# A hybrid decoder layer on one core: a group's value products start with the one that needs the last masked copy

## The chip, the cores and the metric

The kernel runs on one core of one Trainium2 chip. The metric is the device time of one execution in microseconds (us). A core has a matrix engine (TensorE, PE in the profile; its weight loads are listed apart as PEld), VectorE (DVE), ScalarE (ACT), GpSimd (POOL) and SyncE (SP), which issues most transfers. Each engine works through its own list of instructions in order and waits on semaphores for the others. Matrix products are written to banks of an accumulation memory called PSUM; DVE and ACT copy them out.

## The reference, cut to what matters

One decoder layer for 2048 tokens of width 1024, in float32. A normalised input is projected into two groups of heads: four recurrent heads (HGRN2) and eight attention heads with two key/value heads. Their outputs are joined, projected and added to the input, then a gated feed-forward part with a short convolution follows, and a last normalisation. The change lies in the attention:

```python
scores = einsum('bnqhgd,bnkhd->bnhgqk', qb, kb) * scale     # a block of 128 queries, 256 keys
scores = where(mask, scores, -inf)                          # causal, window of 128
m = maximum(max(scores, -1), sink)
p = exp(scores - m)
denom = sum(p, -1) + exp(sink - m)
out = einsum('bnhgqk,bnkhd->bnqhgd', p / denom, vb)         # the value products
```

Each block of 128 queries reads its own block of 128 keys and the previous one. The first block of all has no previous one.

## The kernel before, in words

The sequence is worked in two halves of 1024 tokens (`hf` 0 and 1). In each half come the mixing part (the heads), the output projection, the feed-forward products and the down projection. The mixing part lies at about 110 to 380 us and 1190 to 1460 us of the profile. In it, four rounds (`h`, `j` = 0 to 3) pair one recurrent head (`hgrn`, a generator) with one pair of attention heads (`attend`, a generator too: one head of key/value head 0, one of key/value head 1); `hymba_layer` advances the two in turn.

`attend` works on groups of four blocks of 128 queries: `g` = 0 and 1 in a half. So there are 16 groups in all: 2 halves, 4 rounds, 2 groups. For a group, the last part of `attend` does this:

- for each key/value head `kv`, four transposes of the probabilities (L497, tile `ppt`), into one of the two PSUM banks of the pool called "at";
- from that bank two masked copies on DVE (L500): `po`, with the mask of the own block, and `pp`, with the mask of the previous one. A group thus has four masked copies, and DVE makes them in the order po and pp of `kv` 0, po and pp of `kv` 1. The last one is pp of `kv` 1;
- the value products (L508) into one bank of "at" (tile `poT`): for each of the four blocks `i` up to two products (own, previous) for each of the two `kv`, 16 in a group, and 14 in the first group of a round in half 0. The product of `kv` 0 fills partitions 0 to 63 of the bank, that of `kv` 1 fills 64 to 127; own and previous are summed in the bank;
- a copy of the bank by ACT (L512, and L518 in round 3, where DVE also makes a low part, L519). What it writes is read by the output projection of that half.

In the profile every product is two records of LDWEIGHTS and two of MATMUL.

All of the rest of TensorE's work in this part are projections (`unit`, L214: 48 matrix products of 128x512 each, tiles named `f`, `hq`, `q`, `g`, and `pop` for the output projection), and the recurrent head's own products (tiles `pdiag`, `plev`, `pkn`, `pu`, `po` of L671 and L672, `pot`). The masked copy `po` of L500 and the tile `po` of L671 and L672 have one name in the profile and are told apart by their lines.

The order on each engine is not that of the text. A planner plays the traced program through a model of time, gives an engine that is free the earliest traced instruction that is ready in that model, and writes down the order; semaphores are put in afterwards. `tc.issue_after(x)` adds that the instructions traced inside it stand behind `x` on `x`'s engine, without a wait. So a projection of the next head fills TensorE where the model says that the value products aren't ready; at run time the written order holds, whatever is ready then.

Of the kernel before, what the change touches and what calls it, by code (L numbers as in the profile page):

```python
# [17 lines left out]
P = 128  # L18
# [32 lines left out]
def hymba_layer(ctx: ExitStack, tc: tile.TileContext, a: dict, out: bass.AP):  # L51
    nc = tc.nc
# [17 lines left out]
    def ps(kind, name):  # L70
        return spaces[kind].tile([P, 512], F32, tag=kind, name=name)
# [3 lines left out]
    def halves():  # L75
        return [(b, slice(b * 512, (b + 1) * 512)) for b in range(NB)]
# [119 lines left out]
    def unit(src, X, name, order=range(KT), kind="mm", then={}, behind={}, in_turn=False):  # L196


        hi, lo = src if isinstance(src, tuple) else prep(src)
        o = [ps(aux[b] if kind == "aux" else kind, f"{name}{b}") for b in range(NB)]  # L200
        order, mark = list(order), None
        for both in [[h] for h in halves()] if in_turn else [halves()]:
            for i, kt in enumerate(order):
                if i in then:
                    then[i]()
                wh, wl = hi[:, kt * P:(kt + 1) * P], lo[:, kt * P:(kt + 1) * P]
                xh, xl = X[kt]
                if i in behind:
                    mark = marks[behind[i]].ins
                with tc.issue_after(mark) if mark else ExitStack():  # L210
                    for w, x, f, l in ((wh, xh, kt == order[0], False), (wh, xl, False, False),
                                       (wl, xh, False, kt == order[-1])):
                        for b, bs in both:
                            marks["unit"] = nc.tensor.matmul(o[b], w, x[:, bs], start=f, stop=l)  # L214
        return o

    def new_x():
        return (xp.tile([P, HALF], F32R, tag="xh", name="XH", bufs=KT),
                xp.tile([P, HALF], F32R, tag="xl", name="XL", bufs=KT))
# [74 lines left out]
    def slot(name):  # L294
        return hp.tile([P, HALF], F32, tag="m", name=name, bufs=KT)
# [102 lines left out]
    def rows(kv):  # L398
        return slice(kv * HD, (kv + 1) * HD)
# [32 lines left out]
    def attend(hf, j, X, invb, KS, V, mix, p):  # L432

        o = unit(a["w_att"][j], X, "q")
        qT = slot(f"att{j}")
        for b, bs in halves():
            nc.vector.scalar_tensor_tensor(qT[:, bs], o[b], 0.125, invb[:, bs], op0=ALU.mult, op1=ALU.mult)
            nc.scalar.activation(qT[:, bs], qT[:, bs], AF.Identity, bias=C.bq[:, j:j + 1])
        yield
        scs = []  # L440
        for g in range(NB):
            sc = p.tile([P, 2, 4, P], F32, tag="sc", name="sc", bufs=2)
            gs = slice(g * 512, (g + 1) * 512)
            for kv in range(2):
                r, other = rows(kv), rows(1 - kv)

                qh, ql = [p.tile([P, 512], F32R, tag="pp", name=n, bufs=4) for n in ("qh", "ql")]
                nc.scalar.copy(qh[r], qT[r, gs])
                nc.scalar.copy(qh[other], qT[r, gs])
                nc.vector.tensor_tensor(ql[r], qT[r, gs], qh[r].bitcast(F32), op=ALU.subtract)  # L450
                nc.scalar.copy(ql[other], ql[r].bitcast(F32))
                for i0 in (0, 2):
                    pb = ps("at", "psc")
                    first = hf == 0 and g == 0 and i0 == 0
                    for i in range(2):
                        n = g * 4 + i0 + i
                        w0 = 1 if first and i == 0 else 0
                        o = pb[:, i * 256 + w0 * P:(i + 1) * 256]
                        ks = slice((n + w0) * P, (n + 2) * P)
                        for t, qx in enumerate((qh, ql)):  # L460
                            nc.tensor.matmul(o, qx[:, (i0 + i) * P:(i0 + i + 1) * P], KS[:, kv, ks],
                                             start=t == 0, stop=t == 1)
                    pv = pb.rearrange("p (i w k) -> p i w k", i=2, w=2)
                    dst = sc[:, kv, i0:i0 + 2]
                    if first:
                        nc.vector.memset(dst[:, 0], NEG)
                        nc.scalar.copy(dst[:, 1], pv[:, 1, 0])
                    else:
                        nc.scalar.copy(dst, pv[:, :, 0])
                    nc.vector.copy_predicated(  # L470
                        dst, C.own.bitcast(U32).unsqueeze(1).to_broadcast([P, 2, P]), pv[:, :, 1])
            m = p.tile([P, 2, 4], F32, tag="mx", name="m", bufs=2)
            nc.vector.tensor_reduce(m.rearrange("p a b -> p (a b)"),
                                    sc.rearrange("p a b c -> p (a b) c"), axis=AX.X, op=ALU.max)
            sk = C.sinkb[:, j].unsqueeze(2).to_broadcast([P, 2, 4])
            nc.vector.tensor_tensor(m, m, sk, op=ALU.max)
            es = p.tile([P, 2, 4], F32, tag="es", name="es", bufs=2)
            nc.vector.tensor_tensor(es, sk, m, op=ALU.subtract)
            nc.vector.tensor_scalar(m, m, -1.0, None, op0=ALU.mult)
            den = p.tile([P, 2, 4], F32, tag="den", name="den", bufs=2)  # L480
            for kv in range(2):
                for i in range(4):
                    nc.scalar.activation(sc[:, kv, i], sc[:, kv, i], AF.Exp, bias=m[:, kv, i:i + 1],
                                         accum_out=den[:, kv, i:i + 1])
            nc.scalar.activation(es, es, AF.Exp)
            nc.vector.tensor_tensor(den, den, es, op=ALU.add)
            nc.vector.reciprocal(den, den)
            nc.vector.tensor_tensor(sc, sc, den.unsqueeze(3).to_broadcast([P, 2, 4, P]), op=ALU.mult)
            scs.append(sc)
        yield  # L490
        for g, sc in enumerate(scs):
            pm = []
            for kv in range(2):
                pm.append([p.tile([P, 4, P], F32, tag="pp", name=n, bufs=4) for n in ("po", "pp")])
                pt = ps("at", "ppt")
                for i in range(4):
                    nc.tensor.transpose(pt[:, i * P:(i + 1) * P], sc[:, kv, i], ident)  # L497
                ptv = pt.rearrange("p (i q) -> p i q", i=4)
                for dst, mk in zip(pm[kv], (C.ownT, C.prevT)):
                    nc.vector.tensor_tensor(dst, ptv, mk.unsqueeze(1).to_broadcast([P, 4, P]), op=ALU.mult)  # L500
            oT = ps("at", "poT")
            for i in range(4):
                n = g * 4 + i
                noprev = hf == 0 and n == 0
                for prev in range(1 if noprev else 2):
                    for kv in range(2):
                        r = rows(kv)
                        nc.tensor.matmul(oT[r, i * P:(i + 1) * P], V[:, n + 1 - prev, r], pm[kv][prev][:, i],  # L508
                                         start=prev == 0, stop=noprev or prev == 1)
            gs = slice(g * 512, (g + 1) * 512)  # L510
            if j < ATT_J - 1:
                nc.scalar.copy(qT[:, gs], oT)  # L512
                mix[4 + j] = qT
            else:
                if g == 0:
                    mix[4 + j] = new_x()
                h, l = mix[4 + j]
                nc.scalar.copy(h[:, gs], oT)  # L518
                nc.vector.tensor_tensor(l[:, gs], oT, h[:, gs].bitcast(F32), op=ALU.subtract)  # L519
            yield  # L520
# [674 lines left out]
    for hf in range(NH):  # L1195
        X, kv, invb, rs, f0 = nxt
        with ExitStack() as st:
            p = pool(f"mix{hf}", stack=st, reuse_waits="tile")
            KS, V = att_keys(hf, kv, invb, p)
# [3 lines left out]
            for h in range(HG):  # L1203
                hg = hgrn(hf, h, X, invb, vs, WG, mix, p, f0 if h == 0 else None)
                at = attend(hf, h, X, invb, KS, V, mix, p)
                with tc.issue_after(summed.ins) if hf + h == 0 else ExitStack():
                    next(hg)
# [28 lines left out]
        with ExitStack() as st:  # L1236
            p = pool(f"ffn{hf}", stack=st, reuse_waits="tile")
            kept, ops, hs, first, last = out_proj(hf, M, p)
# [63 lines left out]
```

## Time and profile before

| what | us |
|---|---|
| time of the kernel, median of 3 runs | 2175.64 (2173.93 to 2177.19) |
| the profiled execution, time | 2174.83 |
| the profiled execution, span from the first to the last instruction | 2173.1 |
| TensorE busy in 1190 to 1460 us | 266.42 of 270 |
| DVE busy in 1190 to 1460 us | 199.10 of 270 |
| ACT busy in 1190 to 1460 us | 156.88 of 270 |

The span leaves out 1.7 us of the profiled execution. A row of the timeline has the start in us, the time from the first start to the last end of the records that it merges, the engine, line and operation, the tile written and those read, and the number of records (x2). An idle time ahead of the first record and what ended it stand in brackets, where it is long enough. Records on TensorE overlap, because matrix products are pipelined: what one costs is read from its start to the next one's start, not from its duration.

### The profile page before, as it was taken

What the parts mean: (1) busy time and instruction counts of PE and PEld (TensorE: products, weight loads), DVE (VectorE), ACT (ScalarE), POOL (GpSimd) and SP (SyncE); (2) the same over time, 40 slices, a digit from 0 to 9 for tenths busy, and PEclk for the clock granted to TensorE, in tenths of its full rate; (3) what the DMA queues carried; (4) which work ended last, traced back from release to release, by engine and by line L of the source; (5) the groups of instructions that cost most, each with busy time, mean ns of one, the idle gap of its engine ahead of it and who ended that gap; (6) DMA issues with size and microseconds to landing.
All of it is one profiled execution on the core that took longest, in us unless ns stands there. A gap on an engine that the chain in (4) does not pass through costs nothing.

```text
span 2173.1 us, 29038 instructions
## 1 busy us (share of the span) xinstructions
PE 2151.3 (99%) x11136; PEld 1809.6 (83%) x11136; DVE 1659.9 (76%) x2446; ACT 1094.1 (50%) x1902; POOL 6.0 (0%) x28
## 2 busy tenths in 40 slices
PE   9999999999999999999999999999999999999998
PEld 7988987888888888788889889878888888888888
DVE  6677677688887878785866776777978888887766
ACT  6556556564444445335736466555544443444353
POOL 1000000000000000000000000000000000000000
PEclk9999999999999999999999999999999999999999
DMA  4101112413232235964631111124133323259643
GB/s 156 49 30 39 49 40 78 136 59 127 92 126 89 96 117 167 375 223 163 205 127 39 42 37 49 47 70 147 58 116 102 117 82 126 93 190 396 226 142 131
DMA packets 94387, 258.09 MB, mean 119 GB/s; under 512 B 11416, under 2 KB 17576, under 8 KB 94248
## 3 DMA queue, kind: packets, MB, share of 16 engines
q1 hardware_dynamic: 88992, 251.30, 34.2%
q10 hardware_dynamic: 5256, 4.94, 0.8%
q8 instruction: 87, 1.43, 0.3%
q14 instruction: 52, 0.43, 0.1%
HBM read 195.10 MB, written 57.15 MB: 116 GB/s over the span
## 4 chain that ended last, share of the span: by engine, by line
PE 93%; DVE 3%; ACT 2%; DMA 1%; issue 1%; SPq 0%; ACTq 0%; DVEq 0%
PE X L885 7%; PE pop L214 7%; PE X L887 7%; PE X L886 7%; PE hq L214 4%; PE f L214 4%; PE q L214 4%; PE g L214 4%; PE Y L885 4%; PE Y L886 4%; PE Y L887 4%; PE pdx L1098 3%; PE pdx L1096 3%; PE pdx L1097 3%; PE pdy L1096 3%; PE pdy L1097 3%
## 5 line engine op out<-in xcount | busy, mean ns | idle before, releaser
L714 ACT CAST whi<-raw 128x1024 fp32r<-128x1024 f32 x88 | 92.6, 1052 | 109.1 <-PE X L886 68.2
L885 PE MATMUL X<-T,whi 128*128 128x512 f32 x352 | 136.9, 389 | 0.0
L886 PE MATMUL X<-T,whi 128*128 128x512 f32 x352 | 136.9, 389 | 0.0
L887 PE MATMUL X<-T,wlo 128*128 128x512 f32 x352 | 136.9, 389 | 0.0
L980 DVE SCALAR_TENSOR_TENSOR y<-ga,cw,y 128x1024 f32<-128x1024 f32 x88 | 112.4, 1280 | 26.0 <-ACT y L978 26.0
L892 ACT COPY u<-X 128x512 f32<-128x512 f32 x88 | 51.5, 585 | 133.2 <-PE X L887 133.0
L715 DVE TENSOR_TENSOR wlo<-raw,whi 128x1024 fp32r<-128x1024 f32 x88 | 107.2, 1219 | 0.0
L715 DVE TENSOR_TENSOR xld<-raw,xhd 128x1024 fp32r<-128x1024 f32 x72 | 80.9, 1132 | 21.7 <-ACT xhd L714 21.2
L192 ACT CAST whi<-raw 128x1024 fp32r<-128x1024 f32 x57 | 59.9, 1050 | 72.2 <-PE pop L214 28.6
L714 ACT CAST xhd<-raw 128x1024 fp32r<-128x1024 f32 x72 | 69.6, 977 | 47.3 <-DMA raw<-act1T 15.5
L193 DVE TENSOR_TENSOR wlo<-raw,whi 128x1024 fp32r<-128x1024 f32 x57 | 69.2, 1217 | 26.4 <-ACT whi L192 26.3
L214 PE MATMUL pop<-XH,wlo 128*128 128x512 f32 x256 | 85.9, 390 | 0.0
L214 PE MATMUL pop<-XL,whi 128*128 128x512 f32 x256 | 85.2, 390 | 0.0
L214 PE MATMUL pop<-XH,whi 128*128 128x512 f32 x256 | 85.0, 393 | 0.0
L886 PEld LDWEIGHTS X<-T,whi 128*128 128x128 f32 x352 | 66.1, 188 | 13.8
L885 PEld LDWEIGHTS X<-T,whi 128*128 128x128 f32 x352 | 66.1, 188 | 13.7
L887 PEld LDWEIGHTS X<-T,wlo 128*128 128x128 f32 x352 | 66.1, 188 | 13.7
L1096 PE MATMUL pdx<-xhd,hid 128*128 128x512 f32 x192 | 74.5, 392 | 1.9 <-ACT hid L714 1.0
L1097 PE MATMUL pdx<-xld,hid 128*128 128x512 f32 x192 | 74.8, 390 | 0.0
L612 DVE TENSOR_TENSOR QK<-QK,f 128x1024 f32<-128x1024 f32 x56 | 68.5, 1223 | 8.2 <-ACT G L598 7.6
L1098 PE MATMUL pdx<-xhd,lod 128*128 128x512 f32 x192 | 73.7, 389 | 0.0
L706 PE MATMUL pvv<-whi,XH 128*128 128x256 f32 x256 | 72.7, 286 | 0.0
(384 smaller groups left out, 6601.1 us busy)
## 6 DMA issues: line engine op xcount, KB each, us to landing
wr<-in_w_down SPq DMA_DIRECT2D x90, 512.0 KB, 5.5
raw<-in_w_gate SPq DMA_DIRECT2D x44, 512.0 KB, 3.7
raw<-in_w_up SPq DMA_DIRECT2D x44, 512.0 KB, 3.7
raw<-act0T SPq DMA_DIRECT2D x20, 512.0 KB, 3.9
raw<-act1T SPq DMA_DIRECT2D x20, 512.0 KB, 5.7
act0B<-y SPq DMA_DIRECT2D x33, 256.0 KB, 2.2
act1B<-y SPq DMA_DIRECT2D x33, 256.0 KB, 2.8
raw<-in_w_out SPq DMA_DIRECT2D x16, 512.0 KB, 6.2
```

The costliest lines, as they stand in the source:

```text
L193: nc.vector.tensor_tensor(lo, raw, hi.bitcast(F32), op=ALU.subtract)
L214: marks["unit"] = nc.tensor.matmul(o[b], w, x[:, bs], start=f, stop=l)
L706: nc.tensor.matmul(o[:, 0:256], xh[:, t], hi[:, c], start=kt == 0, stop=False)
L714: return (nc.scalar.copy(h, src), (eng or nc.vector).tensor_tensor(l, src, h.bitcast(F32), op=ALU.subtract))
L715: (eng or nc.vector).tensor_tensor(l, src, h.bitcast(F32), op=ALU.subtract))
L885: nc.tensor.matmul(o, wh[:, ws], xh, start=i == 0 and not more, stop=False, skip_group_check=more)
L886: nc.tensor.matmul(o, wh[:, ws], xl, start=False, stop=False, skip_group_check=more)
L887: r = nc.tensor.matmul(o, wl[:, ws], xh, start=False, stop=i == 3, skip_group_check=more)
L980: nc.vector.scalar_tensor_tensor(y, g[:, w:w + HALF], C.cw[:, ft, w:w + 1], y, op0=ALU.mult, op1=ALU.add)
L1096: nc.tensor.matmul(o, wh[:, i, c], ah[:, i, cols], start=f, stop=False, skip_group_check=more)
L1097: nc.tensor.matmul(o, wh[:, i, c], al[:, i, cols], start=False, stop=False, skip_group_check=more)
L1098: nc.tensor.matmul(o, wl[:, i, c], ah[:, i, cols], start=False, stop=l, skip_group_check=more)
```

## The change

The loops over a group's value products run backwards: block 3 first, previous before own, `kv` 1 before `kv` 0. So the first product reads pp of `kv` 1, the last masked copy. All others of the group are put behind it with `issue_after`. The marks that begin and end a sum in the bank follow the new order: previous begins it, own ends it. No instruction is added or taken away.

```diff
             oT = ps("at", "poT")
-            for i in range(4):
+            first = None
+            for i in (3, 2, 1, 0):
                 n = g * 4 + i
                 noprev = hf == 0 and n == 0
-                for prev in range(1 if noprev else 2):
-                    for kv in range(2):
+                for prev in (0,) if noprev else (1, 0):
+                    for kv in (1, 0):
                         r = rows(kv)
-                        nc.tensor.matmul(oT[r, i * P:(i + 1) * P], V[:, n + 1 - prev, r], pm[kv][prev][:, i],
-                                         start=prev == 0, stop=noprev or prev == 1)
+                        with tc.issue_after(first) if first else ExitStack():
+                            mm = nc.tensor.matmul(oT[r, i * P:(i + 1) * P], V[:, n + 1 - prev, r], pm[kv][prev][:, i],
+                                                  start=noprev or prev == 1, stop=prev == 0)
+                        first = first or mm.ins
```

## The prediction, made before the result was known

> **What bounds the kernel now.** The page first: its busy times, and the chain of waits by engine.
>
> ```profile
> PE 2151.3 (99%) x11136; PEld 1809.6 (83%) x11136; DVE 1659.9 (76%) x2446; ACT 1094.1 (50%) x1902; POOL 6.0 (0%) x28
> ...
> PE 93%; DVE 3%; ACT 2%; DMA 1%; issue 1%; SPq 0%; ACTq 0%; DVEq 0%
> ```
>
> TensorE is the bound nearly everywhere, so what counts is how many microseconds of its list the change takes out, and where TensorE itself stands idle. Next, the view of waits for TensorE alone, its two rows on the value products:
>
> ```profile
> PE poT L508 <- DVE pp L500: 3.5, 5, 1.5
> ...
> PE poT L508 <- DVE po L500: 1.1, 4, 0.4
> ```
>
> Only 4.6 us in all are spent in waiting for masked copies (3.5 + 1.1), and in few places. So the waits can't be most of the matter. The timeline of TensorE shows two kinds of groups. In the 12 groups of rounds 0 to 2, one product stands alone, some projections follow, and then the other 15 (or 13) come in one block. Here is the second group of round 1, half 1, with the last masked copy from DVE's timeline in front:
>
> ```profile
> 1290.26 0.68 DVE L500 TENSOR_TENSOR pp<-ppt,prevT 128x512 f32<-128x512 f32 x1
> ...
> 1290.58 0.63 PE L214 MATMUL hq<-XH,wlo 128*128 128x512 f32 x2
> 1291.04 0.63 PE L214 MATMUL q<-XH,whi 128*128 128x512 f32 x2
> 1291.60 0.43 PE L508 MATMUL poT<-po,V 128*64 128x128 f32 x2
> 1291.96 0.74 PE L214 MATMUL q<-XL,whi 128*128 128x512 f32 x2
> 1292.54 0.63 PE L214 MATMUL q<-XH,wlo 128*128 128x512 f32 x2
> ...
> 1294.95 0.32 PE L508 MATMUL poT<-po,V 128*64 128x128 f32 x1
> ...
> 1296.42 0.48 PE L508 MATMUL poT<-pp,V 128*64 128x128 f32 x3
> 1296.84 0.50 PE L214 MATMUL q<-XL,whi 128*128 128x512 f32 x1
> ```
>
> The reader is to see the single product at 1291.60 (two records), with full-width projections on both sides. The first and the last of the 12 such products are these:
>
> ```profile
> 130.23 0.43 PE L508 MATMUL poT<-po,V 128*64 128x128 f32 x2
> ...
> 1376.58 0.43 PE L508 MATMUL poT<-po,V 128*64 128x128 f32 x2
> ```
>
> In the four groups of round 3 TensorE has no other work and waits step by step. Half 1, first group, then second group; the block ends where the next row of another tile starts:
>
> ```profile
> 1438.74 1.04 PE L497 MATMUL ppt<-ident,sc 128*128 128x128 f32 x8
> 1441.30 0.40 PE L508 MATMUL poT<-po,V 128*64 128x128 f32 x2 [1.52 <-DVE pp L500]
> 1442.06 0.32 PE L508 MATMUL poT<-po,V 128*64 128x128 f32 x1 [0.36 <-DVE po L500]
> ...
> 1442.66 0.32 PE L508 MATMUL poT<-pp,V 128*64 128x128 f32 x1 [0.16 <-DVE pp L500]
> ...
> 1444.33 0.49 PE L671 MATMUL po<-v,ST 128*128 128x128 f32 x2
> ...
> 1451.13 0.32 PE L508 MATMUL poT<-po,V 128*64 128x128 f32 x1 [0.18 <-DVE po L500]
> ...
> 1451.72 0.32 PE L508 MATMUL poT<-pp,V 128*64 128x128 f32 x1 [0.16 <-DVE pp L500]
> ...
> 1453.40 0.50 PE L214 MATMUL pop<-XH,whi 128*128 128x512 f32 x1
> ```
>
> **The change, part by part.** It issues no transfer and touches no queue of SP, ACT or POOL; 248 products stay 248. It alters where in TensorE's list they stand.
>
> *Rounds 0 to 2: the lone product goes.* A full-width pair normally takes 0.46 us from start to start (1290.58 to 1291.04). The pair ahead of the lone product takes 0.56 (1291.04 to 1291.60), the product 0.36 (to 1291.96), the pair behind it 0.58 (to 1292.54). So it costs 0.10 + 0.36 + 0.12 = 0.58 us: its own records are the smaller part, the two passages between wide and 64-column work the rest. With the change no product is ready in the planner's model until the last masked copy is, and then all are; I expect one block of 16. What does the sixteenth cost inside the block? The block of 15 takes 1.89 us (1294.95 to 1296.84), the 13 products after the last wait in round 3 take 1.67 (1442.66 to 1444.33): 0.22 for two. Products of `kv` 0 and 1 run beside each other, and the last one of an odd block has no partner, as the row at 1296.42 shows (three records of pp alone, with no po among them). The sixteenth fills that place: nothing at the low end, half a pair, 0.11, at the high end. I take nothing, because the odd rest is visible. Sum: 12 x 0.58 = **7.0 us** less (5.6 with 0.11 each).
>
> What this leans on is that the block needn't wait. In the group shown, the last copy ended at 1290.94, and its block began at 1294.95, 4.0 us later. The smallest distance is in the first group of round 0:
>
> ```profile
> 127.33 0.68 DVE L500 TENSOR_TENSOR pp<-ppt,prevT 128x512 f32<-128x512 f32 x1
> ...
> 131.35 0.54 PE L508 MATMUL poT<-po,V 128*64 128x128 f32 x5
> ```
>
> It ended at 128.01, 3.3 us ahead. The block may now be placed later by what lies between po and pp of `kv` 1, 0.6 us; projections fill that at no cost, since they have to be done anyway. ACT's copy of the bank moves with it, and what is queued behind it on ACT; nobody needs that copy before the output projection. If the cover were gone, each group would wait for the missing time in full.
>
> *Round 3: the early products lose their cover.* Here the products before the last copy ran in idle time; now all 16 begin behind it. In half 1 the block would start at 1442.66 and take the 1.89 us of eight pairs, so it ends at 1444.55 instead of 1444.33: 0.22 later. The second group: 1451.72 + 1.89 = 1453.61 instead of 1453.40, 0.21. The first group of half 0 had more done early:
>
> ```profile
> 364.07 0.68 DVE L500 TENSOR_TENSOR pp<-ppt,prevT 128x512 f32<-128x512 f32 x1
> ...
> 364.22 0.54 PE L508 MATMUL poT<-po,V 128*64 128x128 f32 x5 [0.36 <-DVE po L500]
> ...
> 366.05 0.38 PE L671 MATMUL po<-v,ST 128*128 128x128 f32 x1
> ```
>
> Its copy ends at 364.75; seven pairs take 1.67, from about 364.81 to 366.48 instead of 366.05: 0.43. With 0.22 for the last group, by the like of half 1: **1.1 us** more. The stall itself doesn't go, it becomes one wait for the last copy: the bracket at 1441.30 grows from 1.52 us to about 2.9 (from 1439.78, the end of the transposes, to 1442.66).
>
> *Does the gain reach the end?* The chain of waits leaves TensorE in half 1 only at 1429.6, behind the last group of round 2, whose block begins at 1382.02, and in half 0 at 318.6, behind the one at 303.94:
>
> ```profile
> 303.94 1.89 PE poT L508 x30
> ...
> 308.10 10.44 PE q L214 x46
> ...
> 318.61 1.05 ACT whi L192
> ...
> 1382.02 1.89 PE poT L508 x30
> ...
> 1429.12 0.49 PE psc L461 x4
> ...
> 1429.63 0.37 ACT sc L469
> ```
>
> So what TensorE saves ahead of these points moves the rest forward, unless ACT or DVE lacks an operand then. I count it in full. **Sum: -7.0 + 1.1 = -5.9 us**, on the profiled execution 2174.83 - 5.9 = 2168.9. The median of the runs is 0.8 above that execution, so 2175.64 - 5.9 = 2169.7.
>
> [...] The longer idle stretch in round 3 could slow TensorE's clock. It is 1.00 there now, but the trace has one drop elsewhere inside the kernel. By the windows view (us; PE, PEld, DVE, ACT and POOL busy; granted clock) and TensorE's timeline around it:
>
> ```profile
> 1430.00:1460.00 30.00, 26.42 (x201) 22.33 (x200) 19.79 (x52) 15.09 (x63) 0.00 (x0) 1.00 0.01 1
> ...
> 1096.36:1099.77 3.41, 3.41 (x10) 2.64 (x9) 3.31 (x15) 1.04 (x1) 0.00 (x0) 0.50 0.12 41
> ...
> 1093.78 1.84 PE L268 MATMUL pst<-ones,invb 128*128 128x1 f32 x16
> ...
> 1097.05 1.05 PE L214 MATMUL kv<-XH,whi 128*128 128x512 f32 x2
> 1097.90 1.05 PE L214 MATMUL kv<-XL,whi 128*128 128x512 f32 x2
> ```
>
> After a few microseconds filled with one-column products the granted clock was 0.50 for 3.41 us, and a pair took 0.85 instead of 0.46: some 1.6 us lost (3.41 x (1 - 0.46/0.85)). In round 3 before, an idle time of 1.52 us brought no such drop. [...] I take no drop and keep it as a rival.
>
> **The rivals.**
>
> - *The clock drops* in round 3 of both halves, at 1.6 us each: -5.9 + 3.2 = -2.7, so 2172.9. For it speaks the row with 0.50; against it, that the clock stayed at 1.00 through the same stretches so far.
> - *Idle time gets filled.* With nothing ready for a while, the planner may put output projections into the waits of round 3 (the bank that held `poT` early is free longer). The brackets of half 1 sum to 2.0 us and 0.3 us; filled in both halves that is 4.6 more: -10.5, so 2165.1. Against it: the same list had no other work there before, and the products behind it are the last ones that projection waits for.
> - *The change doesn't do what it says*: the planner still splits a block, since the products behind the first one are ordered but not tied to it. Then the passages stay and only round 3's loss is left: +1.1, so 2176.7. Against it: once the last copy is there, everything is ready, and the 15 came as one block.
> - *Slower: the one wait takes the place of the passages.* TensorE's list is fixed by the model, and the block now always stands behind the latest of four copies. If DVE's list puts other operations ahead of that copy, the whole of TensorE stands still, projections behind it too. The price of one is in the page:
>
> ```profile
> L612 DVE TENSOR_TENSOR QK<-QK,f 128x1024 f32<-128x1024 f32 x56 | 68.5, 1223 | 8.2 <-ACT G L598 7.6
> ```
>
> It needs 3.3 to 4.0 us of them to use up the cover, and turns the result from 5.9 / 12 = 0.49 us of wait a group. One operation of 1.2 us beyond the cover in all 12: +14.4 - 5.9 = +8.5, so 2184.1. Against it stands the cover.
>
> **How the numbers follow.** Forecast, 2167.5 to 2172: 50 in 100. The lower part of the idle filled, 2163 to 2167: 13. Clock or a gain that ACT and DVE hold up in part, 2171.5 to 2175: 14. Unchanged blocks, about 2176.7: 10. Slower by the wait, 2180 and above: 13. About 0.2%, 4.35 us, is what a measurement of this kernel can tell from no change; that lies at 2171.3. The forecast's own high end (0.11 for each sixteenth product: 2171.1) is close to it, and I give 5 of its 50 to the other side. Faster: 45 + 13 = 58. Within: 5 + 14 + 10 = 29, and one of the last case's, 30. Slower: 12. The range from 2163.5 to 2177 holds the first four cases but for the lowest few.
>
> **What would show it.** Right: in rounds 0 to 2 no `poT` record alone between projections, blocks of 32 (28) records with 1.89 (1.67) us to the next tile, no bracket ahead of them; in round 3 one bracket of some 2.9 and 1.3 us instead of three, and TensorE's waits for po of L500 gone. Wrong: blocks split again; brackets in rounds 0 to 2; a granted clock of 0.50 near 1440; or rows of projection between the transposes and the block of round 3. The planner lays out the whole program anew, so other rows may change their order; a difference far from these groups would speak against my sum even if the total came out.

## The result, and the profile after

| kernel | median, us | runs, us | ratio to before, 95% interval |
|---|---|---|---|
| before | 2175.47 | 2173.89 to 2177.19 (6) | |
| changed | 2169.51 | 2165.41 to 2171.84 (6) | 0.9971 [0.996, 0.9981] |

The change saves 0.29%, 6.3 us by the ratio, with an interval of 4.1 to 8.7. The profiled execution is the slowest of the six: 2171.84 us with a span of 2170.1, so it shows only 3.0 of it against its counterpart. The same parts of the page after the change (the edit moves the line numbers by 2 or 3: the value products are L510 now):

```profile
PE 2143.9 (99%) x11136; PEld 1809.0 (83%) x11136; DVE 1661.1 (77%) x2446; ACT 1094.6 (50%) x1902; POOL 6.0 (0%) x28
...
PE 94%; DVE 3%; ACT 2%; DMA 1%; issue 1%; SPq 0%; DVEq 0%; ACTq 0%
```

The engines work as they did, and TensorE has 7.4 us less of busy time. The view of waits for TensorE (us in total, times, longest):

```profile
PE poT L510 <- DVE m L479: 5.9, 2, 3.0
...
PE pdx L1099 <- DVE y L994: 1.6, 2, 1.1
...
PE poT L510 <- DVE y L172: 1.4, 1, 1.4
PE kv L214 <- DVE y L178: 1.3, 1, 1.3
...
PE poT L510 <- DVE ms L166: 0.8, 1, 0.8
```

The four waits on value products are those of round 3; rounds 0 to 2 have none. The releaser named is the DVE instruction behind the last copy, which began before TensorE went on. Next the group of the prediction (round 1, half 1) in the timeline, again with its last masked copy in front:

```profile
1287.77 0.68 DVE L500 TENSOR_TENSOR pp<-ppt,prevT 128x512 f32<-128x512 f32 x1
...
1291.98 0.62 PE L214 MATMUL q<-XH,whi 128*128 128x512 f32 x2
1292.43 0.61 PE L214 MATMUL q<-XL,whi 128*128 128x512 f32 x2
1292.98 0.44 PE L510 MATMUL poT<-pp,V 128*64 128x128 f32 x4
...
1294.56 0.39 PE L510 MATMUL poT<-po,V 128*64 128x128 f32 x4
1294.88 0.73 PE L214 MATMUL q<-XH,wlo 128*128 128x512 f32 x2
1295.45 0.62 PE L214 MATMUL q<-XH,whi 128*128 128x512 f32 x2
```

No product stands alone: 32 records in one block take 1.90 us (1292.98 to 1294.88), as the 15 products did. The last copy ended at 1288.45, 4.5 us ahead. The passages into and out of 64-column work are paid once now (0.55 and 0.57 for a pair that otherwise takes 0.45).

Four points of the timeline frame rounds 0 to 2, from the first masked copy to the products `pu` of round 3; a fifth is the end of round 3 in half 0. Before:

```profile
124.94 0.68 DVE L500 TENSOR_TENSOR po<-ppt,ownT 128x512 f32<-128x512 f32 x1
...
359.01 2.05 PE L653 MATMUL pu<-v,Kn 128*128 128x128 f32 x16 [1.36 <-ACT Kn L647]
...
375.11 0.50 PE L214 MATMUL pop<-XH,whi 128*128 128x512 f32 x1
...
1202.34 0.68 DVE L500 TENSOR_TENSOR po<-ppt,ownT 128x512 f32<-128x512 f32 x1
...
1436.85 2.05 PE L653 MATMUL pu<-v,Kn 128*128 128x128 f32 x16 [1.10 <-ACT Kn L647]
```

And after, with round 3 of both halves:

```profile
124.92 0.68 DVE L500 TENSOR_TENSOR po<-ppt,ownT 128x512 f32<-128x512 f32 x1
...
355.62 2.05 PE L656 MATMUL pu<-v,Kn 128*128 128x128 f32 x16 [1.35 <-ACT Kn L650]
...
361.51 0.44 PE L510 MATMUL poT<-pp,V 128*64 128x128 f32 x4 [2.97 <-DVE m L479]
...
363.19 0.49 PE L674 MATMUL po<-v,ST 128*128 128x128 f32 x2
...
372.57 0.50 PE L214 MATMUL pop<-XH,whi 128*128 128x512 f32 x1
...
1200.88 0.68 DVE L500 TENSOR_TENSOR po<-ppt,ownT 128x512 f32<-128x512 f32 x1
...
1432.01 2.05 PE L656 MATMUL pu<-v,Kn 128*128 128x128 f32 x16 [1.10 <-ACT Kn L650]
...
1437.90 0.44 PE L510 MATMUL poT<-pp,V 128*64 128x128 f32 x4 [2.97 <-DVE m L479]
...
1440.90 0.80 PE L674 MATMUL po<-v,ST 128*128 128x128 f32 x2
...
1450.25 0.50 PE L214 MATMUL pop<-XH,whi 128*128 128x512 f32 x1
```

From these the span is put together. Rounds 0 to 2 of half 0, from the first masked copy to the products `pu` of round 3: 234.07 before, 230.70 after, -3.37. Half 1: 234.51 and 231.13, -3.38. That is -6.75 for 12 groups, **0.56 each**. Round 3, from `pu` to the first `pop` behind the second block: in half 0 16.10 before (359.01 to 375.11) and 16.95 after, +0.85. In half 1 16.55 before (1436.85 to 1453.40) and 18.24 after, +1.69. The waits `pdx <- y` and `kv <- y` ahead of half 1 are 2.9 us here and were 1.6 before (0.9 and 0.7), which is most of the rest. They are 0.2 us or nothing in all the kernels below, with the new order or without it, and one of those has the very list of the changed kernel, so they are no part of the change. Sum: -6.75 + 0.85 + 1.69 + 1.3 = -2.9, against -3.0 measured.

Half 1's +1.69 hides a block that took 3.00 us (1437.90 to 1440.90) for what took 1.90 above. The windows view of this stretch (us; PE, PEld, DVE, ACT and POOL busy; granted clock, share and rate of the DMAs):

```profile
359.96:363.38 3.42, 1.87 (x29) 1.73 (x30) 3.12 (x9) 1.90 (x10) 0.00 (x0) 1.00 0.00 0
...
1435.16:1438.58 3.42, 0.68 (x13) 0.71 (x15) 3.35 (x10) 0.92 (x5) 0.00 (x0) 1.00 0.00 0
1438.58:1441.99 3.41, 3.41 (x29) 3.08 (x26) 1.80 (x6) 3.02 (x15) 0.00 (x0) 0.50 0.00 0
```

Behind the wait of 2.97 us in half 1 the granted clock was 0.50 for 3.41 us. Behind the equal wait of half 0 it stayed at 1.00 (363.38 to 366.79). Three things were open: whether the 0.56 is the passages, as the prediction had it, or the mere presence of one more product; what round 3 costs; and what decides on the clock.

### The profile page after: what moved, and what is told of

It is laid out like the page before. It is cut to its first block, busy times and chain, and to the rows that moved or that the text cites. A ratio compares the mean times of both kernels' runs of the same rounds, so it can differ in the third digit from the quotient of the medians.

```text
span 2170.1 us, 29025 instructions
## 1 busy us (share of the span) xinstructions
PE 2143.9 (99%) x11136; PEld 1809.0 (83%) x11136; DVE 1661.1 (77%) x2446; ACT 1094.6 (50%) x1902; POOL 6.0 (0%) x28
## 4 chain that ended last, share of the span: by engine, by line
PE 94%; DVE 3%; ACT 2%; DMA 1%; issue 1%; SPq 0%; DVEq 0%; ACTq 0%
PE X L888 7%; PE X L890 7%; PE X L889 7%; PE pop L214 7%; PE hq L214 4%; PE f L214 4%; PE q L214 4%; PE Y L890 4%; PE Y L888 4%; PE Y L889 4%; PE g L214 4%; PE pdx L1101 3%; PE pdx L1099 3%; PE pdx L1100 3%; PE pdy L1100 3%; PE pdy L1099 3%
```

## The experiments

Each edit is shown against the changed kernel. The runs of one set share the runs of the kernel before: 2174.55 us (2171.05 to 2177.52) for the two with one lone product put back, 2174.84 (2170.93 to 2179.09) for the other four. An expectation stands as it was written ahead of the runs.

**The new order in rounds 0 to 2 alone.** Round 3 keeps the order of before.

```diff
-            first = None
-            for i in (3, 2, 1, 0):
+            first, late = None, j < ATT_J - 1
+            for i in (3, 2, 1, 0) if late else range(4):
...
-                for prev in (0,) if noprev else (1, 0):
-                    for kv in (1, 0):
+                for prev in (0,) if noprev else (1, 0) if late else (0, 1):
+                    for kv in (1, 0) if late else (0, 1):
...
-                                                  start=noprev or prev == 1, stop=prev == 0)
-                        first = first or mm.ins
+                                                  start=noprev or prev == late, stop=noprev or prev != late)
+                        first = first or mm.ins if late else None
```

> The change in rounds 0 to 2 alone, the old order in round 3. Theory (the passages between wide and 64-column products are the whole gain, round 3 only costs): 12 blocks of 16 (14) products in one piece, -6.8 to -7.0 us, about 2168.6; round 3 waits in three steps of 1.52, 0.36 and 0.16 us again, no granted clock of 0.50 in it, and times that spread less than those of the changed kernel (2165.4 to 2171.8). Rival (round 3 is where the time comes from, or the new order of the whole program): no faster than 2173.

Measured: 2168.26 us (2164.61 to 2170.27, 9 runs), ratio 0.9969 [0.9959, 0.9978]: -6.7 us. The view of waits has the rows of before again:

```profile
PE poT L510 <- DVE pp L500: 3.5, 5, 1.5
...
PE poT L510 <- DVE po L500: 1.1, 4, 0.4
```

No clock drop lies in round 3 of its profile. The gain of the rounds 0 to 2 alone is thus 6.7 us by time and 6.75 by rows. That this kernel would spread less was a miss: 5.7 us from lowest to highest against 6.4. Four of its nine runs took 2164.6 to 2165.6 us at a mean granted clock of 0.999 or 1.000, the other five 2168.3 to 2170.3 at 0.997 or 0.998. So here too the longer runs are those with the lower clock, although the waits of round 3 are the old ones.

**The new order in round 3 alone.** As above, with the other condition.

```diff
-            first, late = None, j < ATT_J - 1
+            first, late = None, j == ATT_J - 1
```

> The change in round 3 alone; rounds 0 to 2 keep a lone product and a block of 15 (13). Theory: slower by 1.1 to 1.7 us (four groups of 0.2 to 0.5 us) without a drop of the clock, by up to 3.2 us more where it drops behind the wait of 2.97 us: 2176.6 to 2180. Rival (the three waits of round 3 were a cost that one wait saves): not slower than 2175.5.

Measured: 2176.75 us (2172.16 to 2179.25, 11 runs), ratio 1.0012 [1.0003, 1.0021]: +2.6 us, from 0.7 to 4.6. So this part of the change is a loss by itself. Its profiled execution was the fastest of the 11 and has no clock drop before TensorE's work is over; half 1 in its timeline:

```profile
1434.48 2.05 PE L656 MATMUL pu<-v,Kn 128*128 128x128 f32 x16 [1.16 <-ACT Kn L650]
...
1440.38 0.44 PE L510 MATMUL poT<-pp,V 128*64 128x128 f32 x4 [2.97 <-DVE m L479]
...
1442.28 0.49 PE L674 MATMUL po<-v,ST 128*128 128x128 f32 x2
...
1451.12 0.50 PE L214 MATMUL pop<-XH,whi 128*128 128x512 f32 x1
```

The wait is 2.97 us as in the changed kernel, the block takes 1.90. From `pu` to the first `pop` behind the second block it is 16.64, +0.09 against before, where the changed kernel had +1.69: the drop cost 1.6 us there. By time, rounds 0 to 2 and round 3 add up: -6.7 + 2.6 = -4.1.

**The order without the tie to the first product.**

```diff
-                        first = first or mm.ins
```

> The loops run backwards as in the change, but nothing is put behind the first product. The written order of all five engines is that of the changed kernel, so both theories expect its time: the theory that the order alone matters 2169.5, within its spread of 2165.4 to 2171.8. A time outside it would mean that two programs of one order differ by more than the runs of one do.

Measured: 2169.95 us (2165.14 to 2172.09, 11 runs), ratio 0.9981 [0.9972, 0.999]: -4.1 us. The planner wrote the same list for all five engines as with `issue_after`. So the order of the loops does everything, and these runs are further runs of the changed kernel in effect. In its profiled execution the clock dropped behind both long waits (windows view, columns as above):

```profile
357.12:360.53 3.41, 1.14 (x11) 0.90 (x9) 3.41 (x10) 0.21 (x1) 0.00 (x0) 1.00 0.00 0
360.53:363.94 3.41, 2.71 (x26) 2.74 (x28) 2.27 (x7) 2.75 (x15) 0.00 (x0) 0.50 0.00 0
1432.32:1435.73 3.41, 0.77 (x14) 0.80 (x16) 3.34 (x10) 1.01 (x6) 0.00 (x0) 1.00 0.00 0
1435.73:1439.14 3.41, 3.41 (x28) 3.08 (x25) 1.80 (x6) 2.85 (x14) 0.00 (x0) 0.50 0.00 0
```

**One lone product put back, 64 columns wide.** Rounds 0 to 2 get one more product ahead of the block. What it writes is overwritten by the block.

```diff
             oT = ps("at", "poT")
+            if j < ATT_J - 1:
+                w = rows(0)
+                nc.tensor.matmul(oT[w, 0:P], V[:, g * 4 + 1, w], pm[0][0][:, 0], start=True, stop=True)
```

> The changed kernel with one product more in each of the 12 groups of rounds 0 to 2: a copy of block 0's own product of key/value head 0, 64 columns of weights, ahead of the block and not tied to it; the block's own products write over it. It is ready with the first masked copy, so it stands alone between projections, as the first product did before. Theory (a lone 64-column product costs 0.57 us, nearly all of it in the passages): 12 x 0.57 = +6.8 over the changed kernel (2169.7), 2176.5, the time of the kernel before or a little over; pieces of 0.10 + 0.36 + 0.11 us in the timeline. Rival (a product costs its 0.11 us wherever it stands, the gain came from elsewhere): +1.3, 2171.

Measured: 2174.53 us (2171.74 to 2180.15, 11 runs), ratio 1.0001 [0.9992, 1.001]. The gain is gone. In its timeline the extra product is L504, here in a group of half 1:

```profile
1214.62 0.71 PE L214 MATMUL hq<-XH,whi 128*128 128x512 f32 x2
1215.26 0.43 PE L504 MATMUL poT<-po,V 128*64 128x128 f32 x2
1215.62 0.73 PE L214 MATMUL hq<-XL,whi 128*128 128x512 f32 x2
1216.20 0.62 PE L214 MATMUL hq<-XH,wlo 128*128 128x512 f32 x2
```

**The same product, 128 columns wide.** Twice the output, the same place, also overwritten.

```diff
-                w = rows(0)
+                w = slice(0, P)
```

> As extra_narrow, but the additional product takes 128 columns of weights (both heads' values). Theory (what costs is the passage between 128-column and 64-column work): its own two records take 0.22 us, like a pair of L671, and leaving float32 work for a projection 0.08, as behind the transposes: 0.3 x 12 = +3.6, 2173.3. Rival (what costs is that any float32 product stands alone between projections, whatever its width): +6.8 as with the narrow one, 2176.5.

Measured: 2169.69 us (2168.69 to 2172.12, 11 runs), ratio 0.9979 [0.997, 0.9987], and the same group in its timeline:

```profile
1212.72 0.71 PE L214 MATMUL hq<-XH,whi 128*128 128x512 f32 x2
1213.27 0.38 PE L504 MATMUL poT<-po,V 128*128 128x128 f32 x2
1213.41 0.71 PE L214 MATMUL hq<-XL,whi 128*128 128x512 f32 x2
1213.96 0.63 PE L214 MATMUL hq<-XH,wlo 128*128 128x512 f32 x2
```

By rows, the wide product has twice the output and costs 0.23 us in this group: 0.14 to the next start, and 0.09 more than 0.46 for the pair behind it. The narrow one costs 0.57: 0.36 to the next start, 0.12 for the pair behind it, and 0.09 for the pair ahead (0.64 against 0.55). By rows that is 12 x 0.34 = 4.1 us between the two kernels, by time 0.0022, or 4.8. All 12 groups together, measured as above from the first masked copy to `pu` in both halves, take 6.47 us more than in the changed kernel with the narrow product and 2.53 more with the wide one: 0.54 and 0.21 each. So most of the price (0.34 of 0.57 us in this group) is the passage between 64-column and 128-column work, not the product. What TensorE does during it, these rows don't show.

The time of the wide kernel was forecast at 2173.3, and that was a miss. At 2169.69 it is no slower than the changed kernel (2169.51, and 2169.95 without the tie), so the 0.21 to 0.23 rest on the rows alone. That the two kernels with a lone product differ is shown by time too: their intervals lie apart.

**Round 3's long wait broken by filler.** Ahead of each block of round 3 four products of ones by ones go into the bank, with no reader.

```diff
             oT = ps("at", "poT")
+            if j == ATT_J - 1:
+                without_use(oT, 4)
```

> The changed kernel with four products of ones by ones per group of round 3, into the bank of the value products, ahead of the block; nothing reads them. They can start when pp of head 0 has been read out of the way, and take some 0.9 us in all (0.22 us each). Theory (the wait of 2.97 us is what lets the clock drop, and the drop costs 1.1 to 1.6 us each time): no granted clock of 0.50 near 360 and 1440, block unchanged in place, so the runs come out at the fast end of the changed kernel's, 2165 to 2168. Rival (the clock has no part in the spread): 2169.5, the same spread, or slower by what the products add.

Measured: 2165.49 us (2165.14 to 2170.09, 6 runs), ratio 0.9969 [0.9958, 0.9981]. The filler begins where the bank is handed on, 1.52 us after the transposes:

```profile
1436.67 1.13 PE L96 MATMUL poT<-ones 128*128 128x128 f32 x8 [1.52 <-DVE pp L500]
1438.04 0.44 PE L512 MATMUL poT<-pp,V 128*64 128x128 f32 x4 [0.23 <-DVE pp L500]
...
1439.93 0.49 PE L676 MATMUL po<-v,ST 128*128 128x128 f32 x2
```

The stall is broken up, the block takes 1.89, and no drop lies in round 3 of its profile. One profile is little to go by, since four of the ten waits of 2.97 us below had no drop either. Five of the six runs took 2165.1 to 2167.0 us, as expected, where 1 of the 11 runs without the tie did. The sixth, 2170.09, is the profiled one: its clock dropped elsewhere, at 10.24 us and, for 6.83 us, at 1092.26. This kernel and that of the first experiment have the lowest ratio of all, but their intervals overlap that of the change, so neither is shown to beat it.

**What decides on the clock.** The drops of one execution lie on a grid. Those of the kernel without the tie begin at 360.53 and 1435.73, 1075.20 us apart, which is 315 times 3.4133, to the rounding the length of a drop (3.41 in the rows). In every other profile with more than one drop they lie whole multiples of it apart as well, to 0.01 us: 1093.83, 1438.58 and 2165.62 in the changed kernel (101 and 213 times), 10.24, 1092.26, 1095.68 and 2164.05 with the filler (317, 1 and 313), 364.09 and 2166.33 with the narrow product (528), 362.13, 1437.33 and 2164.37 with the wide one (315 and 213). So each execution can be cut into stretches of 3.413 us, and TensorE's idle time counted in the one ahead. Ten waits of 2.97 us were profiled; this is the stretch with the most idle time around each:

| kernel | half 0: idle us, then | half 1: idle us, then |
|---|---|---|
| changed | 1.55, no drop | 2.74, drop |
| round 3 alone | 1.88, no drop | 1.61, no drop |
| without the tie | 2.27, drop | 2.64, drop |
| lone narrow product | 2.50, drop | 1.59, no drop |
| lone wide product | 2.47, drop | 2.94, drop |

Among these ten waits there are six drops, at 2.27 us and more, and four without one, at 1.88 and less. The row that lies nearest on the side without a drop is that of round 3 alone (3.41 less 1.53 busy):

```profile
360.16:363.57 3.41, 1.53 (x14) 1.29 (x13) 3.41 (x9) 0.21 (x1) 0.00 (x0) 1.00 0.00 0
```

The old order stays below 2.27: its waits in one group sum to 2.04 us (1.52, 0.36 and 0.16), and they would all have to fall into one stretch to reach even that, a value in the open range. In the three profiles with a wait of 1.52 us no stretch of round 3 has over 1.6 us idle, and none has a drop. Where the grid lies is different in each execution (counted from the start of the span, a point of it lies 0.68 us behind a multiple of 3.4133 in the kernel before, 1.57 in the changed one, 2.13 without the tie), so the same wait of 2.97 us costs up to 1.6 us or nothing. In half 1 a drop cost 1.6 us, as worked out above; in half 0 it cost 1.3, as the kernel without the tie took 2.98 us for the first block there (361.23 to 364.21) and the changed kernel, with the same list and no drop, 1.68 (361.51 to 363.19). A wait of length 2.97 leaves at least T in one stretch for a share of (3.41 + 2.97 - 2 x T) / 3.41 of the grid's positions: 0.54 for T = 2.27, 0.77 for 1.88. With T taken as the limit, two such waits at 1.3 and 1.6 us make 1.6 to 2.2 us on average. This is an estimate: it leaves out the shorter idle times around the wait. With the 0.94 us that round 3 costs without drops (0.85 + 0.09), that is 2.5 to 3.2, and round 3 alone measured 2.6.

Idle time by this count is not a rule for the whole program. With the filler, a drop began at 10.24 us behind a stretch with only 1.16 us idle, among the first projections:

```profile
6.82:10.24 3.42, 2.26 (x7) 0.98 (x7) 1.49 (x4) 2.52 (x4) 0.17 (x1) 1.00 1.02 382
10.24:13.65 3.41, 3.16 (x7) 1.97 (x7) 2.99 (x4) 2.74 (x5) 0.00 (x0) 0.50 1.02 416
```

At the end of the program, where TensorE runs out of work, drops followed stretches with 1.73 us idle (lone wide product) and 1.94 us (changed kernel). So the ten waits sort by idle time, but no experiment moved the grid against a wait, and what is counted stays open.

## Why the prediction was right, and where it was not

- **The lone product's passages** (0.58 us each, 7.0 in all): right. 0.56 each by the rows, 6.7 by time with rounds 0 to 2 alone. A narrow product put back takes the gain away, a wide one takes 0.23. That it is the passage was argued from rows in the prediction; the pair of experiments shows that it is the width, and not that a product stands alone.
- **The sixteenth product at nothing:** right. The block took 1.90 for 1.89.
- **The block's cover of 3.3 to 4.0 us:** right. It is 4.5 us in the group shown and 3.6 at least in the 12 groups, and rounds 0 to 2 have no wait. So the slower rival, one wait in place of the passages, didn't come.
- **Round 3's 1.1 us for the early products:** the sum without drops is 0.94, its parts were off. The four waits (2.97, 1.38, 2.97, 0.84) were forecast as 2.9 and 1.3. In half 0 it was +0.85 instead of 0.65: behind these waits the block starts 0.14 us after its copy (361.37, where the last copy ended, to 361.51) and 0.15 in the second group, not 0.06. In half 1 without a drop it was +0.09 instead of 0.43: the planner put two of six `pop` products behind the second group's transposes instead of ahead.
- **"I take no drop":** this step failed. The clock dropped behind 6 of 10 long waits. The prediction had the drop as a rival, in both halves and at 1.6 us each. The size was about right (1.6 us in half 1, 1.3 in half 0), and in the profiles it came in some half of the cases. The wait of 1.52 us in the kernel before, without a drop, didn't speak for one of 2.97: a stretch with 2.27 us of idle time was followed by a drop.
- **The idle time filled, and the blocks split all the same:** neither came. The only projections in a wait of round 3 are the six `pop` products, which stood there or just ahead of it before.
- **The total:** 2169.7 forecast, 2169.51 measured. The agreement is closer than the parts, and so in part luck. Without drops the parts give -5.8; with drops they give -6.75 + 0.94 + 1.6 to 2.2, so -3.6 to -4.2 on average. The six runs gave -6.3 [-8.7, -4.1], the 11 runs of the same list -4.1 [-6.1, -2.2]. The forecast -5.9 lies in both intervals. The sum with drops lies in the second and only touches the first.

What stays open: whether such waits have a limit between 1.88 and 2.27 us, and what decides on a drop elsewhere. The drop in the prediction came after products of one column with no idle time on TensorE (3.41 of 3.41 us busy from 1092.95 to 1096.36), and another after 1.16 us of it, so the idle time is not all that counts.

## What to carry to other kernels

On an engine that is the bound, look for single instructions of another shape between long runs of one shape, and read their price from start to start, passages included: here 0.57 us for a product whose wide twin costs 0.23. Delaying such an instruction until its whole block is ready paid where other work fills the time (-6.7 us in rounds 0 to 2), and cost 2.6 us where none did (round 3). Where the engine stands idle anyway (round 3), start what is ready: keep the old order there, for the work that it hides (0.94 us here, without drops), and because it breaks a long wait into pieces (1.52, 0.36 and 0.16 us for 2.97, with no drop in round 3 of the two profiles with the old order there).

## What the runs showed of the hardware beyond that

A stall of TensorE can cost more than its length: behind 2.97 us of waiting the granted clock was halved for the next 3.41 us in 6 of 10 cases, at 1.3 to 1.6 us where the cost could be read. Whether it was went with where the stall fell on a grid of 3.41 us that shifts from one execution to the next: in the ten cases a stretch with 2.27 us or more of idle time was followed by a drop, one with 1.88 or less was not. With nothing changed, runs of one kernel differ along with the granted clock: the fastest of the 11 without the tie took 2165.14 us at a mean of 0.999, the slowest 2172.09 at 0.997. Drops are not confined to round 3: the kernel before dropped at 1096.36, and its runs also spread over 8 us (2170.93 to 2179.09).
